# Swapping two buffers in SBUF, and moving split rests, block differences and half-row squares between engines, in a two-layer decoder trunk

## The chip, the cores and the metric

The kernel runs on one core of a Trainium2 chip. The metric is device time in microseconds (us) of one execution; a kernel is run several times and the median is taken. Engines are called by the names that the profile's rows use: PE is TensorE, DVE is VectorE, ACT is ScalarE, POOL is GpSimd, SP is SyncE, which here only issues DMA transfers.

## The reference

x is 1024 tokens by 1024 features in float32. Two layers follow each other; the attention functions themselves are left out here.

```python
def rmsnorm(x, g):
    y = x32 * lax.rsqrt(jnp.mean(x32 * x32, axis=-1, keepdims=True) + RMS_EPS)
    return y * g

def swiglu(h, w_up, w_down):                     # hidden size 2816
    a, b = jnp.split(h @ w_up, 2, axis=-1)
    return (jax.nn.silu(a) * b) @ w_down

for layer in range(2):
    h = rmsnorm(x, norm_mix[layer])
    if layer == 0:                               # "A": compressed + selected + sliding window branches
        mix = nsa_attention(h, a_w_in, ..., a_w_out, rel_bias)
    else:                                        # "B": three (window, dilation) groups, shared K and V
        kv = rmsnorm(x, kv_norm) @ kv_w          # reshaped to three dilations, K and V, 4 groups of 64
        mix = dilated_attention(h, b_w_q, k_shared, v_shared, b_w_out, rel_bias)
    x = x + mix
    x = x + swiglu(rmsnorm(x, norm_ffn[layer]), ffn_w_up[layer], ffn_w_down[layer])
return rmsnorm(x, final_norm)
```

There are 16 heads of 64, in 4 groups. The dilated attention has queries for three dilations (1, 4, 16), all projected from the stream after layer 0.

## The kernel before, in words

**Numbers in two parts.** Every large product is taken on float32 values that are split in two: a rounded high part and the rest. `Pairs` (L993 to L1004) makes such a pair: ScalarE copies the high part (`ph`, L1002), and VectorE, or another engine that is passed as `eng`, subtracts it from the source (`pl`, L1003). `split` does the same into given tiles (L348, L349). A product is then three matmuls (`mm3`, L375 to L377): high by high, and the two mixed ones.

**Products in blocks.** The dense matrices are multiplied in 2 by 2 blocks of 512 with seven products instead of eight. `Blocks` holds the seven left operands made of the normalised stream, transposed and split: B11, B21 (first half of the rows), T1 to T4 and B22 (sums and differences of blocks). `Blocks.factor` gives a row's reciprocal root mean square: the first 512 columns are squared and summed by ScalarE (L1103), the second 512 by VectorE (L1104), then the two sums are added. `Blocks.half` (from L1128) scales the rows, and `make` (L1157 to L1178) forms T1 to T4, with differences by `minus` (L1163), whose even rows go to VectorE and odd rows to GpSimd. `cols_steps` (from L1199) gives the seven products m1 to m7 of one weight block: each splits its weights by `pairs` and multiplies them by one operand; m1 uses B11, m2 B21, m5 T1, m6 T2, m7 T3, m4 T4 and m3 B22.

**The dense part of a layer** is `dense` (L1516 to L1534). It keeps the residual stream in `xr`, 128 partitions by 8 rows by 1024 (32 KB of a partition, pool "fx"). `out_proj` (L1295 to L1350) multiplies the attention's output with w_out; its weights k = 4 to 7 are loaded straight into the four upper rows of xr, the others into a pool of their own (`ow`, loads at L1313). When its last first-half step is done, B11 and B21 are allocated in pool "fb" (also 32 KB). `ffn` (L1371) then runs `hidden` for j = 0 to 21, 128 hidden columns each: weights arrive by DMA, GpSimd multiplies them by the norm's gains (L1388), GpSimd forms the block sums (L1236, L1237, L1251, L1253), and the seven products follow; the down projection is accumulated into xr by VectorE (L1061, and L1506 for the last). For the first three j, `eng` is GpSimd in m1 and m2.

**Between the layers.** `project_B` (L1543 to L1668) runs 18 jobs (6 of keys and values, 12 of queries), each again the seven products, on operands made from the stream after layer 0; `begin_B` (L1536) makes the first half of them during the down projection. It uses xr's rows in pairs as space (`chunk`) in which finished queries are split (L351, L352), from where GpSimd's queue writes them to memory (`qB`, L1592). For its first two jobs `eng` is GpSimd.

**The dilated attention** (L1673 to L1916) then opens pools in the places that have come free: T12 (bias tiles), Q1, K1 for the wide dilations, and so on. `load_first` (L1695) loads the first group in three slices, in SyncE's order: T12 (L1730, L1731), then for each slice Q1, K1, V1, Q2, K2, V2 (L1704, L1710, L1712), later Q0, K0, V0 and T0 for the near dilation (dilation 1). L1793 and L1798 are the first products of keys and queries of the wide groups, L1813 those of the near one. After it a merge (L1857 to L1876) adds the three dilations by weight.

**Order.** Inside the attentions a hand-written order is used. The rest is ordered by a scheduler that simulates a timeline, so that instructions of one engine stand in the order that it found; a tile that is placed where another lay waits for the last use of the other.

Of the kernel before, what the change touches and what calls it, by code (L numbers as in the profile page):

```python
# [299 lines left out]
def trunk(ctx, tc, I, out):  # L300
    nc = tc.nc

    def pool(c, name, side="left", space=None):
        if space is not None:
            return c.enter_context(tc.tile_pool(name=name, bufs=1, space=space,
                                                **({} if space is DR else {"reuse_waits": "tile"})))
        return c.enter_context(tc.tile_pool(name=name, bufs=1, side=side, reuse_waits="tile"))
# [785 lines left out]
    class Blocks:  # L1093
# [5 lines left out]
        def factor(self, xt, junk):  # L1099
            lo, hi = slice(0, 512), slice(512, 1024)  # L1100
            ss = cst.tile([128, 2], F32, name="nss2", bufs=8)
            rs = ss[:, 0:1]
            nc.scalar.activation(junk[0], xt[:, lo], AF.Square, accum_out=rs)  # L1103
            nc.vector.tensor_tensor_reduce(out=junk[1], in0=xt[:, hi], in1=xt[:, hi], scale=1.0, scalar=0.0,  # L1104
                                           op0=OP.mult, op1=OP.add, accum_out=ss[:, 1:2])
            nc.vector.tensor_add(rs, rs, ss[:, 1:2])
            nc.scalar.activation(rs, rs, AF.Sqrt, bias=eps, scale=1.0 / D)
            nc.vector.reciprocal(rs, rs)
            return rs
# [48 lines left out]
        def make(self, name):  # L1158
            (a, b), t = self.x1, self.t
            first = lambda j, h: self.xr[:, j, h * 512:(h + 1) * 512]  # L1160

            def minus(o, x, y, j):
                (nc.vector, nc.gpsimd)[j % 2].tensor_sub(o, x, y)  # L1163

            if name == "T1":
                for j in range(4):
                    nc.vector.scalar_tensor_tensor(t[j], first(j, 0), self.less[j], a[j], op0=OP.mult, op1=OP.add)
                self.turned(name, t)
                for j in range(4):
                    minus(a[j], b[j], a[j], j)  # L1170
            elif name == "T2":
                for j in range(4):
                    minus(t[j], b[j], t[j], j)
                self.turned(name, t)
            elif name == "T3":
                self.turned(name, a)
                for j in range(4):
                    nc.vector.scalar_tensor_tensor(a[j], first(j, 1), self.rs[j], t[j], op0=OP.mult, op1=OP.subtract)  # L1178
            else:
                self.turned(name, a if name == "T4" else b)  # L1180
# [114 lines left out]
    def out_proj(c, near, far, B, xr, oT, w, x_src, late):  # L1295
# [38 lines left out]
        def first(k):  # L1334
            def prep():
                a = pairs(oT[:, k, lo])
                for c_ in range(2):
                    split(*ops[k][c_], raw[k][:, c_ * 512:(c_ + 1) * 512])
                return a

            def run(a):
                a = [part(a, t) for t in range(4)]
                for cs in (((0,), (1,)) if k == 0 else ((0, 1),)):
                    products(k, a, range(4), cs)
                if k == 7:
                    for t in range(4, NT):
                        rows(t)
                    cr.close()
                    B.add(pool(c, "fb", far), ("B11", "B21"))
            return step(prep, run)  # L1350

        def later(m, k):
# [18 lines left out]
    def ffn(p, scratch, B, xr, layer):  # L1371
# [27 lines left out]
        def hidden(j, u):  # L1399

            def ahead(f):
                if j == 1:
                    raw[2].clear()
                if 0 < j < NJ - 1:
                    for q in range(3):
                        load_up(j + 1, q)
                return f()

            def tmp(n):
                if n in ("d0", "d1"):  # L1410
                    return u[base + int(n[1])]
                return scratch[15] if (j, n) == (0, "c") else misc[n]

            def done(a, r, C):
                t = u[base + r]
                if a == 0:
                    nc.scalar.activation(t, C, AF.Silu)
                else:
                    nc.vector.tensor_mul(t, t, C)

            base = 2 * (j % 2)
            banks = {0: ("dx2", "uy", "uy"), 1: ("dx3", "ux", "uy")}.get(j, ("ux", "uy", "uy"))
            steps = cols_steps(banks, "m1 m2 m5 m6 m7 m4 m3", pairs, tmp, B.ops, lambda: raw[j], done,
                               eng=nc.gpsimd if j < 3 else None)
            i = 2 if j in (1, 2) else 0
            steps[i] = steps[i][0], lambda f=steps[i][1]: ahead(f)

            def m4(f=steps[5][1]):
                if j == 0:
                    raw[1].clear()  # L1430
                if j + 1 < NJ:
                    for q in range(3 if j else 0, 4):
                        load_up(j + 1, q)
                return f()
            steps[5] = "m4", m4
            return steps
# [79 lines left out]
    def dense(layer, w, x_src, oT, tail, near, far):  # L1516

        lo, hi = slice(0, 512), slice(512, 1024)
        scratch = [oT[:, 4 * b + i, h] for h in (lo, hi) for b in range(2) for i in range(4)]
        with ExitStack() as c:  # L1520
            c.push(open_banks(*[(n,) for n in ("dx0", "dx1", "dx2", "dr0", "dr1", "ux", "dx3", "uy")]))
            B = Blocks()
            xr = pool(c, "fx", far).tile([128, NT, D], F32, name="xr")
            out_proj(c, near, far, B, xr, oT, w, x_src, layer and 7)
            with ExitStack() as cu:
                p = pool(cu, "fu", near)
                with ExitStack() as ch:
                    B.add(pool(ch, "fb2", far), second)
                    last = ffn(p, scratch, B, xr, layer)
                with ExitStack() as ch:  # L1530
                    pz = pool(ch, "fz", far)
                    begin, finish = tail
                    last(pz, *begin(pz, B, xr))
            finish(c, B, xr, scratch)  # L1534
# [8 lines left out]
    def project_B(c, B, xr, scratch):  # L1543
# [97 lines left out]
        def steps(n):  # L1641
            done = tokens_out(n) if jobs[n][0] == "v" else rows_out(n)
            s = cols_steps((("ux", "uy")[n % 2], "dr0", "dr1"),
                           "m1 m2 m6 m5 m7 m4 m3" if n else "m1 m2 m5 m6 m7 m4 m3", pairs, tmp_of(n), B.ops,
                           lambda: raw[n], done, view_of(n), nc.gpsimd if n < 2 else None)

            def third(f=s[2][1]):
                if 0 < n < len(jobs) - 1:
                    load(n + 1)
                return f()  # L1650
            s[2] = s[2][0], third
            return s
# [318 lines left out]
```

## Time and profile before

| what | value |
|---|---|
| median of 3 runs | 2940.07 us (2934.08 to 2941.08) |
| the profiled execution's own time | 2943.19 us |
| its span (first to last instruction) | 2941.4 us |
| granted TensorE clock, mean over the span | 0.986 |
| PE busy | 2827.1 us (96%) |
| DVE busy | 2266.9 us (77%) |
| POOL busy | 1586.8 us (54%) |
| ACT busy | 1509.1 us (51%) |
| moved by DMA | 294.46 MB, 100 GB/s over the span |

Times inside the profile are counted from the start of the span. A row of a timeline gives the start, the duration, engine, line and operation, with "out<-in" by the names of the tiles; in square brackets stands the idle time of the engine ahead of it and what ended that. A row of waits gives engine, operand and line, what released it, and then total us, number and longest. In the operands, h and l mark the high part and the rest. oT and oTb are big buffers (the attention's output, later used in pieces as space for weights), so that many temporary tiles carry these names. The stages of the span in short: attention A to about 700, dense part of layer 0 to about 1440, project_B to about 1847, the dilated attention to about 2175, the dense part of layer 1 to the end.

### The profile page before, as it was taken

Reading aid. Unit: us, or ns where it says so; the run is one execution under the profiler, and the core shown is the slowest. Engines: PE = TensorE matmul, PEld = TensorE weight load, DVE = VectorE, ACT = ScalarE, POOL = GpSimd, SP = SyncE. Lnnn points to the kernel's source line nnn. Section 1 sums busy time; section 2 is a strip of 40 time slices with the busy share of each in tenths; the row PEclk is TensorE's granted clock in tenths of the full one; section 3 lists DMA queues with packets and bytes.
Section 4 is the critical chain, followed back from the end, with each engine's and each line's share of the span. In section 5 each row is a group of like instructions: output and inputs, shape, how many; then the busy total and the mean of one; then the engine's idle time right before and its main releaser. Section 6 shows DMA issues by size and latency. Waiting matters only on the chain.

```text
span 2941.4 us, 43840 instructions
## 1 busy us (share of the span) xinstructions
PE 2827.1 (96%) x14766; PEld 2377.7 (81%) x14766; DVE 2266.9 (77%) x4485; ACT 1509.1 (51%) x3266; POOL 1586.8 (54%) x1804
## 2 busy tenths in 40 slices
PE   7999999999999999999899999699999999999997
PEld 6988999998877888888678788588878778888886
DVE  5441999996588889888866776489975888898887
ACT  5431888886443333333444444589854433333334
POOL 2134777773365555555456786355523655555551
PEclk8999999999999999999999999899999999999999
DMA  6756243202123222321224554766521221112112
GB/s 160 234 160 189 60 109 88 75 10 115 33 75 74 71 65 61 83 61 54 97 93 140 160 164 141 233 198 194 159 88 33 72 61 51 54 50 62 54 43 76
DMA packets 266833, 294.46 MB, mean 100 GB/s; under 512 B 18099, under 2 KB 209475, under 8 KB 266608
## 3 DMA queue, kind: packets, MB, share of 16 engines
q1 hardware_dynamic: 246960, 231.50, 27.2%
q0 software_dynamic: 19648, 60.16, 6.8%
q8 instruction: 117, 1.92, 0.3%
q14 instruction: 108, 0.88, 0.1%
HBM read 228.49 MB, written 78.81 MB: 104 GB/s over the span
## 4 chain that ended last, share of the span: by engine, by line
PE 69%; DVE 16%; ACT 4%; issue 4%; DMA 4%; POOL 3%; SPq 1%; DVEq 0%; POOLq 0%; ACTq 0%
PE ux L375 5%; PE ux L376 5%; PE ux L377 5%; DVE pl L1003 5%; PE pt L485 4%; PE uy L375 4%; PE uy L376 4%; PE uy L377 4%; DVE xr L1061 4%; PE dx L376 3%; PE dx L377 3%; PE dr L375 3%; PE dx L375 3%; PE dr L376 3%; PE mm L375 3%
## 5 line engine op out<-in xcount | busy, mean ns | idle before, releaser
L1003 DVE TENSOR_TENSOR pl<-oT,ph 128x512 fp32r<-128x512 f32 x315 | 314.9, 1019 | 74.8 <-ACT ph L1002 69.0
L1002 ACT ACTIVATE ph<-oT 128x512 fp32r<-128x512 f32 x325 | 196.4, 626 | 219.3 <-PE ux L376 59.9
L485 PE MATMUL pt<-ident,P 128*128 128x128 f32 x1536 | 260.0, 277 | 5.1 <-DVE tl L349 2.5
L1003 DVE TENSOR_TENSOR pl<-oTb,ph 128x512 fp32r<-128x512 f32 x229 | 216.8, 971 | 52.0 <-ACT ph L1002 47.1
L1002 ACT ACTIVATE ph<-oTb 128x512 fp32r<-128x512 f32 x235 | 140.6, 625 | 189.9 <-PE ux L376 52.4
L1061 DVE TENSOR_TENSOR xr<-xr,dr 128x512 f32<-128x512 f32 x320 | 204.5, 678 | 27.9 <-PE dr L377 27.9
L1388 POOL TENSOR_TENSOR oT<-oT,gffn 128x512 f32<-128x512 f32 x92 | 108.7, 1188 | 199.9 <-DMA oT<-in_ffn_w_up_dram 185.1
L349 DVE TENSOR_TENSOR tl<-pt,th 128x512 fp32r<-128x512 f32 (+1 forms) x320 | 194.2, 625 | 15.4 <-ACT th L348 13.3
L485 PEld LDWEIGHTS pt<-ident,P 128*128 128x128 f32 x1536 | 181.4, 141 | 28.3 <-POOL P L924 4.1
L924 POOL TENSOR_SCALAR P<-P,sm,gates 128x384 f32<-128x384 f32 (+7 forms) x256 | 182.7, 724 | 37.8 <-DVE sm L922 31.8
L1061 DVE TENSOR_TENSOR xr<-xr,dx 128x512 f32<-128x512 f32 x320 | 200.0, 678 | 2.5 <-PE dx L377 1.8
L348 ACT ACTIVATE th<-pt 128x512 fp32r<-128x512 f32 (+1 forms) x320 | 168.4, 546 | 40.0 <-PE pt L485 31.0
L1388 POOL TENSOR_TENSOR oTb<-oTb,gffn 128x512 f32<-128x512 f32 x92 | 103.8, 1136 | 151.6 <-DMA oTb<-in_ffn_w_up_dram 135.6
L920 ACT ACTIVATE P<-P,m 128x384 f32<-128x384 f32 (+7 forms) x256 | 171.1, 671 | 12.5 <-DVE m L918 9.0
L376 PE MATMUL dx<-pl,ph 128*128 128x512 f32 x384 | 152.7, 398 | 0.9
L1762 ACT ACTIVATE P<-P,st 128x384 f32<-128x384 f32 (+2 forms) x256 | 139.5, 548 | 26.1 <-DVE st L1757 25.1
L377 PE MATMUL dx<-ph,pl 128*128 128x512 f32 x384 | 149.9, 393 | 0.4 <-DVE pl L1003 0.4
L1757 DVE CUSTOM_DVE_ANT_0 P<-s,T 128x384 f32<-128x384 f32 (+2 forms) x256 | 115.6, 478 | 37.8 <-PE s L1798 26.9
L510 PE MATMUL o<-tl,V 128*128 128x256 f32 x476 | 135.8, 302 | 0.0
L509 PE MATMUL o<-th,V 128*128 128x256 f32 x476 | 135.1, 298 | 0.2 <-DVE oTb L522 0.2
L375 PE MATMUL dx<-ph 128*128 128x512 f32 x384 | 117.2, 398 | 6.7 <-DVE xr L1506 4.9
L1002 ACT ACTIVATE ph<-wd 128x512 fp32r<-128x512 f32 x86 | 53.8, 629 | 115.7 <-PE ux L376 55.0
(924 smaller groups left out, 9546.1 us busy)
## 6 DMA issues: line engine op xcount, KB each, us to landing
qB<-xr POOLq DMA_DIRECT2D x96, 256.0 KB, 4.7
oT<-in_ffn_w_up_dram SPq DMA_DIRECT2D x92, 256.0 KB, 3.1
oTb<-in_ffn_w_up_dram SPq DMA_DIRECT2D x92, 256.0 KB, 3.1
Q<-qB SPq DMA_DIRECT2D x40, 512.0 KB, 7.3
wd<-in_ffn_w_down_dram SPq DMA_DIRECT2D x66, 256.0 KB, 2.6
oT<-in_b_w_q_dram SPq DMA_DIRECT2D x48, 256.0 KB, 3.3
K<-kBs SPq DMA_DIRECT2D x40, 256.0 KB, 9.6
wraw<-in_a_w_in_dram SPq DMA_DIRECT2D x18, 512.0 KB, 4.7
```

The lines of the kernel that those rows point to most:

```text
L348: nc.scalar.activation(H_, src, AF.Copy)
L349: nc.vector.tensor_sub(L_, src, f32(H_))
L375: nc.tensor.matmul(ps, lh, rh, start=first, stop=False, skip_group_check=bool(shared))
L376: nc.tensor.matmul(ps, lh, rl, start=False, stop=False, skip_group_check=bool(shared))
L377: return nc.tensor.matmul(ps, ll, rh, start=False, stop=last, skip_group_check=bool(shared))
L485: nc.tensor.transpose(ps[:, i * 128:(i + 1) * 128], b, ident)
L920: nc.scalar.activation(P[:, e, :n], P[:, e, :n], AF.Exp, bias=mm[:, e:e + 1], scale=-1.0, accum_out=sm[:, e:e + 1])
L924: nc.gpsimd.tensor_scalar(P[:, e, :n], P[:, e, :n], sm[:, e:e + 1], gt(g, t, br, 2 * hp + e, 1), op0=OP.mult, op1=OP.mult)
L1002: nc.scalar.activation(like(h), src, AF.Copy)
L1003: (eng or nc.vector).tensor_sub(like(l), src, f32(like(h)))
L1061: nc.vector.tensor_add(xs, xs, banks[t])
L1388: nc.gpsimd.tensor_mul(v, v, gains[:, k:k + 4].unsqueeze(2).to_broadcast([128, 4, 128]))
```

## The change

It has five edits. (1) `factor` squares both halves of a row on ScalarE. (2) `minus` uses VectorE for all rows; 12 differences of a run move from GpSimd. (3) In `hidden` for j = 0 to 2 and in (4) `project_B` for n = 0 and 1, the rests of m1's and m2's weights are made by VectorE as everywhere else: 16 operations, 12 of them in the two ffn parts. (5) Pool "fb" with B11 and B21 is opened in `dense` ahead of "fx" and no longer in `out_proj`, so that the two 32 KB regions change places. In layer 0 (right side) xr goes from byte 163392 of a partition to 130624 and B11/B21 the other way; in layer 1 (left side) xr goes from 50496 to 83264. In the dilated attention T12, Q1 and K1 lie from 165440 to 196160, Q0 and K0 from about 130240.

```diff
@@ -1101,8 +1101,7 @@
             ss = cst.tile([128, 2], F32, name="nss2", bufs=8)
             rs = ss[:, 0:1]
             nc.scalar.activation(junk[0], xt[:, lo], AF.Square, accum_out=rs)
-            nc.vector.tensor_tensor_reduce(out=junk[1], in0=xt[:, hi], in1=xt[:, hi], scale=1.0, scalar=0.0,
-                                           op0=OP.mult, op1=OP.add, accum_out=ss[:, 1:2])
+            nc.scalar.activation(junk[1], xt[:, hi], AF.Square, accum_out=ss[:, 1:2])
             nc.vector.tensor_add(rs, rs, ss[:, 1:2])
             nc.scalar.activation(rs, rs, AF.Sqrt, bias=eps, scale=1.0 / D)
             nc.vector.reciprocal(rs, rs)
@@ -1160,7 +1159,7 @@
             first = lambda j, h: self.xr[:, j, h * 512:(h + 1) * 512]
 
             def minus(o, x, y, j):
-                (nc.vector, nc.gpsimd)[j % 2].tensor_sub(o, x, y)
+                nc.vector.tensor_sub(o, x, y)
 
             if name == "T1":
                 for j in range(4):
@@ -1346,7 +1345,6 @@
                     for t in range(4, NT):
                         rows(t)
                     cr.close()
-                    B.add(pool(c, "fb", far), ("B11", "B21"))
             return step(prep, run)
 
         def later(m, k):
@@ -1420,8 +1418,7 @@
 
             base = 2 * (j % 2)
             banks = {0: ("dx2", "uy", "uy"), 1: ("dx3", "ux", "uy")}.get(j, ("ux", "uy", "uy"))
-            steps = cols_steps(banks, "m1 m2 m5 m6 m7 m4 m3", pairs, tmp, B.ops, lambda: raw[j], done,
-                               eng=nc.gpsimd if j < 3 else None)
+            steps = cols_steps(banks, "m1 m2 m5 m6 m7 m4 m3", pairs, tmp, B.ops, lambda: raw[j], done)
             i = 2 if j in (1, 2) else 0
             steps[i] = steps[i][0], lambda f=steps[i][1]: ahead(f)
 
@@ -1520,6 +1517,7 @@
         with ExitStack() as c:
             c.push(open_banks(*[(n,) for n in ("dx0", "dx1", "dx2", "dr0", "dr1", "ux", "dx3", "uy")]))
             B = Blocks()
+            B.add(pool(c, "fb", far), ("B11", "B21"))
             xr = pool(c, "fx", far).tile([128, NT, D], F32, name="xr")
             out_proj(c, near, far, B, xr, oT, w, x_src, layer and 7)
             with ExitStack() as cu:
@@ -1642,7 +1640,7 @@
             done = tokens_out(n) if jobs[n][0] == "v" else rows_out(n)
             s = cols_steps((("ux", "uy")[n % 2], "dr0", "dr1"),
                            "m1 m2 m6 m5 m7 m4 m3" if n else "m1 m2 m5 m6 m7 m4 m3", pairs, tmp_of(n), B.ops,
-                           lambda: raw[n], done, view_of(n), nc.gpsimd if n < 2 else None)
+                           lambda: raw[n], done, view_of(n))
 
             def third(f=s[2][1]):
                 if 0 < n < len(jobs) - 1:
```

Removed lines shift the later ones: the numbers after the change are smaller by one from L1105 on, by two from L1348, by three from L1423 to L1520, and by two behind that.

SyncE at the start of the dilated attention, with what each load waits for (DMAHW and DMASW are counters of transfers issued by SyncE and by GpSimd, the others of engines; oT is the last weight load of project_B; s1 and s2 hold bias in memory). Before:

```order
L1568 DMA oT_2477<-in_b_w_q_dram 128x4x128 [waits DMAHW2_49,DVE_49]
L1682 DMA rows_19095<-in_rowsel_dram 128x512 [waits DMAHW3_49,PE_49]
L1730 DMA T120_19103<-s1_80 128x256 [waits DMASW4_49,DMASW5_49,DMASW3_49,DMASW6_49,DMASW2_49,DMASW7_49,DMASW1_49,DMAHW4_49,DMASW0_49,DVE_49]
L1731 DMA T120_19103<-s2_81 128x128 [waits DMAHW5_49]
L1730 DMA T121_19106<-s1_80 128x256 [waits DMAHW6_49]
```

The same place after the change:

```order
L1566 DMA oT_2477<-in_b_w_q_dram 128x4x128 [waits DMAHW2_49,DVE_49]
L1728 DMA T120_19103<-s1_80 128x256 [waits DMAHW3_49,PE_49]
L1729 DMA T120_19103<-s2_81 128x128 [waits DMAHW4_49]
L1728 DMA T121_19106<-s1_80 128x256 [waits DMAHW5_49,PE_49]
L1729 DMA T121_19106<-s2_81 128x128 [waits DMAHW6_49]
```

The first bias load waited for GpSimd's eight counters, that is for the last writes of qB, and for VectorE's last split into xr; now it waits for a matmul. The counter numbers resolve to the last job's m1 (`uy<-B11`) for T120 and T121; Q10 to Q13 wait for two further reads of B11 and for older writes of qB; V10 waits for the last `pl<-oT` on VectorE, and Q0 for the last writes of qB. The load of `rows` stands behind the first group's key slices. In layer 0's dense part the first w_out load waits for the last product of the attention instead of an earlier one; in layer 1's, the four loads of w_out into xr wait for GpSimd's last L1876.

VectorE at the end of layer 0 (dx_15273 is a sum of the second last down projection into xr, dx_15717 and on those of the last; xn and nss are a row's scratch and its sum of squares). Before:

```order
L1061 TENSOR_TENSOR xr<-xr,dx_15273 128x512
L1003 TENSOR_TENSOR pl<-oT,ph 128x512 x3
L1419 TENSOR_TENSOR oT<-oT 128x512
L1003 TENSOR_TENSOR pl<-s_16151,ph 128x512
L1003 TENSOR_TENSOR pl<-oT,ph 128x512
L1506 TENSOR_TENSOR xr<-xr,dx_15717 128x512
L1506 TENSOR_TENSOR xr<-xr,dx_15725 128x512
L1506 TENSOR_TENSOR xr<-xr,dx_15734 128x512
L1506 TENSOR_TENSOR xr<-xr,dx_15742 128x512
L1104 ISA xn_15685,nss_15793<-xr 128x512
L1104 ISA nss_15793 128x1
L1506 TENSOR_TENSOR xr<-xr,dx_15751 128x512
```

After:

```order
L1061 TENSOR_TENSOR xr<-xr,dx_15273 128x512
L1003 TENSOR_TENSOR pl<-oT,ph 128x512 x3
L1417 TENSOR_TENSOR oT<-oT 128x512
L1003 TENSOR_TENSOR pl<-oT,ph 128x512 x4
L1003 TENSOR_TENSOR pl<-s_16151,ph 128x512
L1003 TENSOR_TENSOR pl<-oT,ph 128x512
L1503 TENSOR_TENSOR xr<-xr,dx_15717 128x512
L1503 TENSOR_TENSOR xr<-xr,dx_15725 128x512
L1503 TENSOR_TENSOR xr<-xr,dx_15734 128x512
L1503 TENSOR_TENSOR xr<-xr,dx_15742 128x512
L1105 TENSOR_TENSOR nss_15793<-nss_15793 128x1
L1503 TENSOR_TENSOR xr<-xr,dx_15751 128x512
```

The four rests that GpSimd made for project_B's first two jobs stand in VectorE's queue ahead of the last sums into xr, and behind the sums the square of the first row is gone.

GpSimd in the first ffn steps of layer 0 (gffn is the norm's gain, tb and wd are space for sums, here of T1's rows). Before:

```order
L1388 TENSOR_TENSOR oT<-oT,gffn_72 128x512
L1003 TENSOR_TENSOR pl<-oT,ph 128x512 x6
L1163 TENSOR_TENSOR tb<-oT,tb 128x512
L1251 TENSOR_TENSOR oT<-oT 128x512
L1163 TENSOR_TENSOR wd_10439<-oT,wd_10439 128x512
L1253 TENSOR_TENSOR oT<-oT 128x512
```

After:

```order
L1235 TENSOR_TENSOR oT<-oT 128x512
L1236 TENSOR_TENSOR oT<-oT 128x512
L1386 TENSOR_TENSOR oT<-oT,gffn_72 128x512
L1250 TENSOR_TENSOR oT<-oT 128x512
L1252 TENSOR_TENSOR oT<-oT 128x512
```

The six rests and the differences of `minus` are gone from GpSimd's queue; what is left are gains and block sums. On VectorE the rests stand right behind the scaling of the second half of the rows, ahead of the operations that form T1, and the transposes of T1 stand 12 to 18 matmuls later in TensorE's order. ScalarE's second squares stand right behind the first ones.

## The prediction

> **What bounds the kernel now.** First the page's head and busy shares, then TensorE's own list of waits (engine, waiting operand and line, releaser: total us, times, longest).
>
> ```profile
> span 2941.4 us, 43840 instructions
> PE 2827.1 (96%) x14766; PEld 2377.7 (81%) x14766; DVE 2266.9 (77%) x4485; ACT 1509.1 (51%) x3266; POOL 1586.8 (54%) x1804
> ```
>
> ```profile
> PE s L1793 <- DMA K<-kBs: 18.1, 2, 17.6
> PE s L1798 <- DMA K<-kBs: 3.5, 4, 2.4
> PE dx L375 <- ACT ow00h L348: 3.1, 1, 3.1
> PE o L509 <- POOL thp L502: 2.8, 3, 2.3
> PE dx L1120 <- DVE T1l L349: 2.1, 1, 2.1
> ```
>
> TensorE is busy for 96% of the span: the change takes no matmul away, so all it can win is the 114 us in which TensorE isn't busy, and the time in which it is busy at a low clock. One wait is large: 17.6 us on the first keys of layer 1's dilated attention. The windows place the waits (stretch, us, then busy us of PE, PEld, DVE, ACT, POOL, the granted clock PEclk, the DMA share, GB/s).
>
> ```profile
> 700.00:704.00 4.00, 3.56 (x10) 2.78 (x11) 4.00 (x8) 3.22 (x7) 0.00 (x0) 0.64 0.98 386
> 1430.00:1440.00 10.00, 4.76 (x19) 3.61 (x19) 10.00 (x9) 1.35 (x3) 8.02 (x5) 0.92 0.10 30
> 1439.20:1445.20 6.00, 5.98 (x14) 4.71 (x15) 4.19 (x10) 3.71 (x8) 2.24 (x3) 0.50 0.58 218
> 1460.00:1490.00 30.00, 24.46 (x119) 18.88 (x118) 27.55 (x46) 14.26 (x28) 14.87 (x12) 0.94 0.21 71
> 1845.00:1865.00 20.00, 2.30 (x9) 1.41 (x7) 2.11 (x4) 3.99 (x6) 4.13 (x8) 0.66 0.68 204
> 2270.00:2290.00 20.00, 15.51 (x80) 11.74 (x79) 19.26 (x25) 11.52 (x20) 13.51 (x10) 1.00 0.18 53
> ```
>
> 1845 to 1865 is the start of the dilated attention: every engine is nearly idle. 1430 to 1440 (end of layer 0), 1460 to 1490 (norms of project_B) and 2270 to 2290 (first steps of layer 1's ffn) are the other kind: VectorE is busy throughout, GpSimd beside it, and TensorE loses 5.2, 5.5 and 4.5 us.
>
> **The swap at the start of the dilated attention.** SyncE's list of waits, SyncE's issues, and the work around them (start us, us, engine, line, operation):
>
> ```profile
> SPq L1730 <- DMA qB<-xr: 18.5, 3, 16.8
> ```
>
> ```profile
> 1823.84 0.39 PE L375 MATMUL uy<-B11h,ph 128*128 128x512 f32 x1
> ...
> 1848.43 2.08 POOL L1592 DMA_DIRECT2D qB<-xr  x4 [1.39 <-ACT xr L351]
> ...
> 1854.77 0.34 SPq L1730 DMA_DIRECT2D T<-s  x1
> ...
> 1858.47 1.85 SPq L1704 DMA_DIRECT2D Q<-qB  x4
> ...
> 1864.39 0.55 PE L1793 MATMUL s<-K,Q 128*128 128x256 f32 x1 [17.64 <-DMA K<-kBs]
> ```
>
> Before, the tiles of T12, Q1 and K1 lie where xr lay, and project_B uses xr's rows as the space from which it writes the finished queries (qB) to memory until the last job. So SyncE stands at its first load until the last write has landed: 1854.77. After, the same tiles lie where B11 and B21 lay. These are last read by the last job's m1 and the product behind it, around 1823.84 to 1826; six more products follow. SyncE then issues T12, Q1 and K1 from about 1824, 30 us earlier. The first value slice follows the last split of the last job, since it lies in the old oT; it, the second group's queries and their first key slice still come before the end of project_B's matmuls. What waits for all qB writes is now Q0, in xr's new place, near the end of that list. The row select load goes behind these too; it was no releaser.
>
> So the 17.64 us go nearly whole. What is late next? The first 16 units' own pace and the near group's bias tile T0, whose load is at the end of the list:
>
> ```profile
> L1793 PE MATMUL s<-K,Q x64: 278/290/580, 1864.4 to 1906.3; 128*128 128x256 f32 x64
> ...
> L1793 PE MATMUL s<-K,Q x64: 276/282/367, 2010.2 to 2053.4; 128*128 128x256 f32 x64
> ```
>
> ```profile
> 1897.14 10.45 DMA T<-sA
> ```
>
> ```profile
> DMA packets 13631, 15.30 MB, mean 251 GB/s; under 512 B 1425, under 2 KB 11025, under 8 KB 13626
> ```
>
> The first wide group took 41.9 us, a later one that waits for no first load 43.2 with other work between: the pace is the kernel's own, so the group moves as a block, and the 17.6 us are kept if T0 comes earlier by as much. It landed at 1907.6 (1897.14 + 10.45), after 15.3 MB at 251 GB/s from 1854 to 1915. With the issue 30 us earlier, less some 9 us in which SyncE stands at the first values, and with the last qB writes in the same queues, I put T0 at 1885 to 1892. That is 16 to 22 us earlier: low end 16. High end 25: the 17.6, the 3.5 and 2.8 us of the two other waits of that attention's start in the list (later keys, T0 by way of GpSimd's thp), and about 1 us for first matmuls at a granted clock of 0.66. I take 20.5: the 17.6 and a little under half of those 6.3 us.
>
> **The swap elsewhere.** At the dense part of layer 0 the first w_out load moves from an earlier matmul's end to that of the attention's last products (matmul, cast that needs the load, group of those loads with KB each and median us from issue to landing):
>
> ```profile
> 695.65 0.28 PE L510 MATMUL o<-tl,V 128*128 128x256 f32 x1
> ```
>
> ```profile
> 699.77 0.61 ACT L348 ACTIVATE ow00h<-ow 128x512 fp32r<-128x512 f32 x1
> ```
>
> ```profile
> ow<-in_a_w_out_dram SPq DMA_DIRECT2D x4, 512.0 KB, 4.2
> ```
>
> 695.93 plus 4.2 is 700.1 against a cast at 699.77, which waits for something else by then; the next three loads go out right behind instead of later. I take 0, bounds 0 and +0.5. At layer 1, xr's new place is under the merge of the three dilations, and four weight loads into it wait for GpSimd's last merge addition:
>
> ```profile
> 2166.45 7.17 POOL L1876 TENSOR_TENSOR oTb<-oTb,o 128x512 f32<-128x512 f32 x4 [2.41 <-DVE oTb L1865]
> ```
>
> ```profile
> 2192.28 0.39 PE L375 MATMUL dx<-ow40h,ph 128*128 128x512 f32 x1
> ```
>
> ```profile
> xr<-in_b_w_out_dram SPq DMA_DIRECT2D x4, 512.0 KB, 5.1
> ```
>
> They are out at 2173.6, land near 2179 and are first used at 2192.28: some 13 us of cover, 0. Without that cover it would cost the 5.1 us of one landing.
>
> **The engine moves.** Sixteen rests and twelve differences go from GpSimd to VectorE, 24 second half-row squares from VectorE to ScalarE. Prices (groups: count, busy us, mean ns): VectorE and GpSimd rests side by side at the end of layer 0, VectorE's rest with GpSimd quiet, and in layer 1's first ffn steps a square on VectorE and the rests on GpSimd.
>
> ```profile
> L1003 DVE TENSOR_TENSOR pl<-oT,ph 128x512 fp32r<-128x512 f32 x4 | 6.1, 1563 | 0.0
> ```
>
> ```profile
> L1003 POOL TENSOR_TENSOR pl<-oT,ph 128x512 fp32r<-128x512 f32 x4 | 6.8, 1727 | 0.0
> ```
>
> ```profile
> L1003 DVE TENSOR_TENSOR pl<-wd,ph 128x512 fp32r<-128x512 f32 x3 | 2.0, 687 | 0.0
> ```
>
> ```profile
> L1104 DVE CUSTOM_DVE_ANT_0 oTb<-xr 128x512 f32<-128x512 f32 x2 | 3.6, 1786 | 0.0
> ```
>
> ```profile
> L1003 POOL TENSOR_TENSOR pl<-oTb,ph 128x512 fp32r<-128x512 f32 x5 | 7.5, 1519 | 17.0 <-PE dr L376 15.5 <-ACT ph L1002 1.6
> ```
>
> A rest takes 0.69 us on VectorE alone and 1.56 beside one of GpSimd: 0.87 for each that meets one. So a moved operation costs VectorE 0.69 and gives up to 0.87 back.
>
> End of layer 0 (VectorE's last residual additions, the matmul that waits for them, ScalarE's first half-row square):
>
> ```profile
> 1438.49 2.47 DVE L1506 TENSOR_TENSOR xr<-xr,dx 128x512 f32<-128x512 f32 x4
> ```
>
> ```profile
> 1439.22 0.79 PE L375 MATMUL dx<-ph 128*128 128x512 f32 x1 [4.87 <-DVE xr L1506]
> ```
>
> ```profile
> 1439.20 0.63 ACT L1103 ACTIVATE xn<-xr 128x512 f32<-128x512 f32 x1 [3.09 <-DVE xr L1506]
> ```
>
> Ahead of the additions at 1438.49, VectorE's four rests at 1.56 become eight at 0.69: 5.5 us instead of 6.3. The two other operations there shed part of their 0.87 each. Bounds -2.5 (both wholly) and +2.75 (four at 0.69 and nothing shed); I take -1.5, since GpSimd keeps two operations there. From 1440 to 1490, eight squares leave VectorE (at 0.69 or more: -5.5), four differences come (+2.75), four differences on GpSimd no longer collide (to -3.5): some 6 us earlier for T1, whose wait is one of those in the 5.5 us that TensorE is idle there. I take -3.3, bounds 0 and -5.5. Sum **-4.8**.
>
> First ffn steps: in 2270 to 2290 two squares at 1.79 leave VectorE (-3.6), five rests and four differences come (9 x 0.69 = +6.2), and nine collisions go (to -7.8): -5.2 on VectorE, and TensorE has 4.5 us to give there. I take -2 in layer 1 and, since layer 0 shows no T1 wait of that size, -1 in layer 0: **-3**, bounds +5 (nothing shed, both layers) and -6.
>
> ScalarE's 24 squares cost 0.63 each and lie where it is busy half of the time (14.26 of 30 us). In layer 0's first norms two squares in line instead of side by side add 0.63 per row, 2.5 over four rows:
>
> ```profile
> 751.54 0.48 DVE L1141 TENSOR_SCALAR oT<-xr,nss 128x512 f32<-128x512 f32 x1
> ...
> 756.60 0.27 PE L1120 MATMUL ux<-ident,oT 128*128 128x128 f32 x1
> ```
>
> The scaled row is there at 752.0, its transpose comes at 756.60: 4.6 us of cover, so 0; uncovered it would be 2.5.
>
> Sum: -20.5 -4.8 -3 = -28.3. The profiled execution took 2943.2 us (span 2941.4); 2943.2 - 28.3 = 2914.9. The median of the runs, 2940.1, lies 3.1 below it, so I forecast 2912.
>
> **The rivals.** (1) The loads, not the distance, bound the start. For it: the DMA share is 0.68 in the very 20 us of the gap, the same bytes must still pass, and SyncE still stands for the values. If bulk loading starts effectively only when that stand ends, the end of the list moves by 12 us instead of 20.5, and with 1 to 3 us from the engine moves the time is 2925 to 2928. Against it: all that the first products need stands in the list ahead of the values. Chance 0.22.
>
> (2) The clock. A gap of 3.1 us (ow00h) is followed by a granted clock of 0.64 over 700 to 704, one of 4.87 us by 0.50 over 1439.2 to 1445.2. If the gap at 1439, shortened to 3.4 us, left the clock full, the six half-clock us there would shrink by 3: 2909. The 0.64 after only 3.1 us speaks against it. Chance 0.08.
>
> The Trainium skill (TensorE: Matmul & The Clock Gate, Part 1: The HAM clock gate) puts the fall to half clock behind at least one idle window of about 3.4 us; by that the shortened gap stands just at the edge, and the trace's 3.1 us gap disagrees.
>
> (3) VectorE becomes the bound, and the kernel is slower. It is busy for 19.26 of 20 us in the first ffn steps. If collisions with GpSimd's remaining operations persist, each of the 28 moved operations costs 1.75 us in front of TensorE, 49 us; the squares give 24 x 0.69 = 16.6 back: +32, less 20.5, is 2952. It is slower than before from 1.33 us for each moved operation ((20.5 + 16.6) / 28). Against it: those collisions are with the very operations that leave. Chance 0.04.
>
> (4) The change doesn't do what it says: SyncE stands, in order, at another load for old qB writes or at Q0, and the keys come as late as before. Then only the engine moves are left: 2940.1 - 8 = 2932, or, with those at half, 2936. Chance 0.04.
>
> **How the numbers follow.** The forecast case has 0.62: its own terms reach from -18 (16, 1.5, 0.5) to -38 (25, 7, 6), 2902 to 2922. With (1) the range goes to 2928; a little below 2902 takes in (2): 2899 to 2928. About 0.3%, 9 us, is what a measurement of this kernel can tell from no change. Faster by more than that: forecast, (1), (2), 0.92; within: (4), 0.04; slower: (3), 0.04.
>
> **What would show it.** Right: SyncE's first T12 load at about 1824 instead of 1854.77; the first product of the dilated attention within 3 us of the end of project_B, with no wait for keys above 3 us and a granted clock near 1 there; the near group 16 to 25 us earlier; gap at the end of layer 0 near 3.4 us. Wrong: that wait still above 8 us, or a new one of TensorE for T0 (GpSimd's select) or for VectorE's rests (pl) in the first ffn steps; a wait for w_out at 700 that grows past 3.6; layer 1's w_out landing after 2192 less the gain.

## The result and the profile after

The changed kernel takes 2913.3 us (median of 4 runs, 2908.86 to 2918.47) against 2940.57 us before (4 runs): 27.3 us less, ratio 0.9911 with a 95% interval of 0.9888 to 0.9934. The forecast was 2912. The profiled execution took 2908.86 us, the fastest of the four, 34.3 us less than the profiled one of before; both traces are single executions, so the trace overstates the gain by some 7 us, and how much of it is clock has to be kept apart.

The first and third line of the page of after:

```profile
span 2907.1 us, 43848 instructions
PE 2817.1 (97%) x14766; PEld 2371.2 (82%) x14766; DVE 2260.1 (78%) x4465; ACT 1522.0 (52%) x3314; POOL 1541.3 (53%) x1776
```

The span is 34.3 us shorter. TensorE's busy time fell by 10.0 us (2827.1 to 2817.1) with the same 14766 matmuls, and the mean granted clock rose from 0.986 to 0.993; its idle time fell by 24.3 us (114.3 to 90.0). TensorE's waits in after:

```profile
PE s L1791 <- DMA K<-kBs: 3.3, 1, 3.3
PE dx L375 <- ACT ow00h L348: 3.1, 1, 3.1
PE o L509 <- POOL thp L502: 2.9, 3, 2.4
...
PE dr L375 <- DVE xr L1061: 2.8, 2, 2.0
...
PE dx L375 <- DVE xr L1503: 2.1, 1, 2.1
...
PE s L1796 <- DMA K<-kBs: 2.0, 2, 1.8
```

The 18.1 us for the first keys are down to 3.3, and the 3.5 us for keys in the next row of products (L1798 before, L1796 after) to 2.0. The wait of 4.9 us at the end of layer 0 is 2.1. The waits for w_out (3.1) and for T0 by way of GpSimd's thp (2.9) stand as before. One wait has grown: that for a residual addition (L1061) is 2.8 us where it was 1.7, and its longest, early in layer 0's ffn, 2.0 where it was 0.8.

SyncE's issues, TensorE's first products and a step of the chain of waits, all of after, at the start of the dilated attention:

```profile
1810.88 0.34 SPq L1728 DMA_DIRECT2D T<-s  x1
...
1814.71 1.75 SPq L1702 DMA_DIRECT2D Q<-qB  x4
...
1819.91 0.38 SPq L1710 DMA_DIRECT2D V<-vBs  x1
```

```profile
1832.75 0.39 PE L377 MATMUL dr<-B22h,pl 128*128 128x512 f32 x1
1832.97 0.88 PE L1791 MATMUL s<-K,Q 128*128 128x256 f32 x6
```

```profile
1866.80 10.44 DMA T<-sA
```

SyncE issues the first bias load 21.9 us ahead of project_B's last matmul, where it stood 8 us behind it before, and the first product of keys and queries follows that last matmul at once. T0 lands at 1877.24. Windows of after, by stage:

```profile
700.00:704.00 4.00, 4.00 (x19) 3.33 (x18) 3.58 (x7) 2.58 (x5) 0.00 (x0) 1.00 1.02 404
1426.00:1436.00 10.00, 6.67 (x25) 4.07 (x26) 10.00 (x17) 3.96 (x9) 5.73 (x3) 1.00 0.09 26
...
1456.00:1486.00 30.00, 28.90 (x143) 23.55 (x142) 29.28 (x49) 17.93 (x36) 8.36 (x8) 0.89 0.21 70
...
1833.00:1848.00 15.00, 10.24 (x71) 9.74 (x70) 8.12 (x24) 11.12 (x27) 5.04 (x10) 0.89 0.90 289
2238.00:2258.00 20.00, 18.34 (x98) 14.39 (x97) 18.20 (x27) 12.06 (x21) 7.03 (x6) 1.00 0.18 53
```

At the end of layer 0 VectorE does 17 operations in 10 us where it did 9, and TensorE is idle 3.3 us instead of 5.2. In project_B's first steps (1456 on) the 5.5 us of idle are 1.1. In layer 1's first ffn steps 4.5 us of idle are 1.7.

### The profile page after: what moved, and what is told of

It is laid out like the page before. It is cut to its first block, busy times and chain, and to the rows that moved or that the text cites. A ratio compares the mean times of both kernels' runs of the same rounds, so it can differ in the third digit from the quotient of the medians.

```text
span 2907.1 us, 43848 instructions
## 1 busy us (share of the span) xinstructions
PE 2817.1 (97%) x14766; PEld 2371.2 (82%) x14766; DVE 2260.1 (78%) x4465; ACT 1522.0 (52%) x3314; POOL 1541.3 (53%) x1776
## 4 chain that ended last, share of the span: by engine, by line
PE 70%; DVE 16%; ACT 4%; issue 4%; DMA 3%; POOL 3%; SPq 1%; DVEq 0%; ACTq 0%; POOLq 0%
PE ux L375 5%; PE ux L376 5%; PE ux L377 5%; PE pt L485 5%; DVE pl L1003 5%; PE uy L375 4%; PE uy L376 4%; DVE xr L1061 4%; PE uy L377 4%; PE dx L376 3%; PE dx L377 3%; PE dr L375 3%; PE dx L375 3%; PE mm L375 3%; PE dr L376 3%
## 5 line engine op out<-in xcount | busy, mean ns | idle before, releaser
L1003 DVE TENSOR_TENSOR pl<-oT,ph 128x512 fp32r<-128x512 f32 x325 | 324.1, 1018 | 71.2 <-ACT ph L1002 61.9
L1061 DVE TENSOR_TENSOR xr<-xr,dr 128x512 f32<-128x512 f32 x320 | 204.5, 678 | 27.6 <-PE dr L377 27.6
L1061 DVE TENSOR_TENSOR xr<-xr,dx 128x512 f32<-128x512 f32 x320 | 199.9, 677 | 2.5 <-PE dx L377 1.8
```

The costliest lines, as they stand in the source:

```text
L1003: (eng or nc.vector).tensor_sub(like(l), src, f32(like(h)))
L1061: nc.vector.tensor_add(xs, xs, banks[t])
```

## The experiments

The theory is that the terms of the prediction add up (the swap at the start of the dilated attention, the engine moves at the end of layer 0 and in the first ffn steps). The rivals that were worth a run: the swap is all of it; the start is bound by the bytes that have to be loaded; of the engine moves one edit carries the gain; the edits trade one wait for another.

### The swap alone

```diff
             B = Blocks()
+            B.add(pool(c, "fb", far), ("B11", "B21"))
...
                     cr.close()
-                    B.add(pool(c, "fb", far), ("B11", "B21"))
```

> Only edit (5): pool fb ahead of fx; every engine move left as before. Theory (terms add up): the whole gain at the start of the dilated attention is the swap's, the first product of keys and queries follows project_B's last matmul within about 3 us, and nothing else moves: 18 us less than before, about 2922, with the gap of 4.9 us at the end of layer 0 still there. Rival A (the swap is nearly the whole change and the engine moves give nothing): 27 us less, about 2913. Rival B (the start is bound by the bytes to be loaded): the first product comes early, but the near group's first product only 12 us earlier, about 2928.

Measured: 2918.9 us, ratio 0.9921 (0.9909 to 0.9934): 21 us less by the medians, 23 by the ratio. Its page and its waits:

```profile
span 2914.1 us, 43853 instructions
PE 2820.5 (97%) x14766; PEld 2375.8 (82%) x14766; DVE 2269.8 (78%) x4485; ACT 1509.2 (52%) x3266; POOL 1585.6 (54%) x1804
```

```profile
PE dx L375 <- DVE xr L1505: 4.9, 1, 4.9
PE o L509 <- POOL thp L502: 4.0, 3, 3.5
PE s L1793 <- DMA K<-kBs: 3.2, 1, 3.2
```

The gap at the end of layer 0 is the old one, the wait for keys the new one. What the swap is worth in its own stage can be read without the rest: from project_B's last matmul to the last product of the near group (L1813 in before, L1811 in after: the source view gives first and last start).

```profile
L1813 PE MATMUL s<-K,Q x256: 274/283/562, 1910.5 to 2151.8; 128*128 128x256 f32 x128
```

```profile
L1813 PE MATMUL s<-K,Q x256: 274/282/562, 1883.6 to 2125.4; 128*128 128x256 f32 x128
```

```profile
L1811 PE MATMUL s<-K,Q x256: 274/283/470, 1879.9 to 2120.2; 128*128 128x256 f32 x128
```

Before, with the last matmul at 1846.36, that is 305.4 us; with the swap alone (last matmul at 1836.40) 289.0; in after (1832.75) 287.5. The swap gives 16.4 to 18 us there. The near group's first product stands 47.2 us behind project_B's last matmul where it stood 64.1, so it comes 16.9 us earlier and not 12: rival B falls. Rival A (nearly everything is the swap) is not borne out, since the moves without the swap give 8 us, next. The 21 to 23 us of the whole runs are 3 to 7 more than the stage shows; no place was found for these.

### The engine moves without the swap

All of the change but edit (5); the diff is that of the change without its two "fb" lines.

> Edits (1) to (4) without the swap. Theory: 9 us less at the end of layer 0 and in project_B's first steps, 3 less in layer 1's first ffn steps, 3 more in layer 0's first ffn steps: about 9 us less than before, 2931, with the 17.6 us wait for keys unchanged. Rival A: no difference beyond 3 us, 2938 to 2943. Rival C (VectorE becomes the bound where GpSimd's work is added): slower than before, 2945 or more.

Measured: 2932.4 us, ratio 0.9971 (0.996 to 0.9982): 8 us less. Its largest wait of TensorE:

```profile
PE s L1791 <- DMA K<-kBs: 17.5, 2, 16.8
```

The wait for keys is untouched. Rivals A and C fall. The theory's sum is right here, but the next six runs show that its parts aren't. This run also gives the swap's price a second time, with the moves on both sides: from project_B's last matmul (1833.54) to the last near product (2141.4) it takes 307.9 us for 287.5 in after, so 20.4 in the stage, and by the medians 19 (2932.4 to 2913.3).

### Squares, rests and differences, one by one and in pairs

```diff
-            nc.vector.tensor_tensor_reduce(out=junk[1], in0=xt[:, hi], in1=xt[:, hi], scale=1.0, scalar=0.0,
-                                           op0=OP.mult, op1=OP.add, accum_out=ss[:, 1:2])
+            nc.scalar.activation(junk[1], xt[:, hi], AF.Square, accum_out=ss[:, 1:2])
```

> Edit (1) alone: both half-row squares on ScalarE. Theory: VectorE's time ahead of the transposes of T1 sets the wait in project_B's first steps, so without eight squares there it gives about 4 us between 1440 and 1490, and 2 in layer 1's first ffn steps; the 4.9 us gap at 1439 stays: 2934. Rival D (the collisions with GpSimd matter, not VectorE's own work): no more than 2 us, 2938 to 2942.

```diff
-            steps = cols_steps(..., done, eng=nc.gpsimd if j < 3 else None)
+            steps = cols_steps(..., done)
...
-                           lambda: raw[n], done, view_of(n), nc.gpsimd if n < 2 else None)
+                           lambda: raw[n], done, view_of(n))
```

> Edits (3) and (4) alone: the 16 rests on VectorE. Theory: the gap of 4.9 us at the end of layer 0 falls by 3 us; in the first ffn steps the rests lengthen VectorE's queue ahead of T1 by 2 to 3 us in each layer, since the squares are still there: about 2 us more to 1 us less, 2939 to 2942. Rival D (collisions matter): VectorE is quicker everywhere, 3 us less in each of three places, about 2931.

```diff
-                (nc.vector, nc.gpsimd)[j % 2].tensor_sub(o, x, y)
+                nc.vector.tensor_sub(o, x, y)
```

> Edit (2) alone: all differences on VectorE. Theory E (of the engine moves, squares and rests alone gave nothing, the two moved together with the differences gave 8 us, so one edit carries it): minus alone gives about 8 us, 2932. Theory I (the three edits work only together, since each alone only trades VectorE's own work against collisions): 0 to 2 us, 2938 to 2941.

The three pairs put two of these edits together each.

> Edits (1), (3) and (4): squares on ScalarE and rests on VectorE, differences shared as before. Theory I: the two are complements (the rests shorten the gap at the end of layer 0 by 3 us, the squares make room for them ahead of T1): 5 to 6 us less than before, about 2934. Theory E: nothing without the differences, 2939 to 2942.

> Edits (1) and (2): squares on ScalarE, differences on VectorE, rests as before. Theory I: project_B's first steps and layer 1's first ffn steps gain 3 us each, the gap at 1439 stays: about 2935. Theory E: all of the 8 us, 2932.

> Edits (2), (3) and (4): differences and rests on VectorE, squares on VectorE too. Theory I: VectorE has 28 operations more and no relief; the gap at 1439 shrinks by 3 us, T1 comes later in three places by 2 us each: 2940 to 2944. Theory E: 8 us less, 2932.

Measured, with two sums of TensorE's waits beside each: the gap at the end of layer 0 (for xr, L1503 to L1506) and all waits for T1's rests (T1l).

| moved | median us | ratio to before (95%) | gap | T1l |
|---|---|---|---|---|
| nothing | 2940.1 to 2940.6 | 1 | 4.9 | 3.6 |
| squares | 2940.3 | 0.9998 (0.9988 to 1.0007) | 4.9 | 3.9 |
| rests | 2942.4 | 1.0005 (0.9996 to 1.0014) | 2.1 | 8.3 |
| differences | 2942.2 | 1.0012 (1.0002 to 1.0022) | 4.9 | 5.8 |
| squares, rests | 2931.8 | 0.9976 (0.9966 to 0.9986) | 2.1 | 1.5 |
| squares, differences | 2942.1 | 1.0008 (1.0 to 1.0017) | 4.9 | 5.0 |
| rests, differences | 2942.5 | 1.0008 (0.9999 to 1.0018) | 2.1 | 8.5 |
| all three | 2932.4 | 0.9971 (0.996 to 0.9982) | 2.1 | 2.1 |

Squares and rests give nothing alone and 8 us together; the differences give nothing in any company and are slower by 0.1% alone, by an interval that just clears 1. For squares alone the theory's 2934 is missed and rival D's 2938 to 2942 holds; for rests alone it is the other way round (2942.4, at the edge of the theory's 2939 to 2942 and far from D's 2931), so neither VectorE's own work nor the collisions account for both. Theory E falls. Theory I holds for two of the pairs (with squares and rests it gave 5 to 6 us, and they are 8) and fails for squares with differences (2935). The two columns on the right show most of why: together they fall from 8.5 to 3.6 us with squares and rests, which is 4.9 of the 8 us, and they rise by 0.3 to 2.2 us in every row that gives nothing. Rows of the waits, of squares alone, rests alone and the pair:

```profile
PE dr L1119 <- DVE T1l L349: 3.1, 2, 1.6
```

```profile
PE dr L1120 <- DVE T1l L349: 6.5, 2, 3.3
```

```profile
PE dr L1119 <- DVE T1l L349: 1.1, 2, 0.6
```

(Two waits each, one in each ffn.) The rests, moved alone, shorten the gap by 2.8 us, but in the ffn they stand in VectorE's queue ahead of T1, together with the squares: the wait for T1 is 3.3 us in each layer, where before it was 1.5 in layer 1 and none in layer 0. The squares, moved alone, leave layer 1's wait where it was and add one of 1.6 in layer 0, which eats what they take from project_B's (2.1 to 0.8). VectorE in layer 1's first ffn steps before (L1104 is a square, L1167 one of the operations of `make` that form T1's rows):

```profile
2265.82 1.77 DVE L1104 CUSTOM_DVE_ANT_0 oTb<-xr 128x512 f32<-128x512 f32 x1
...
2267.60 0.74 DVE L1167 SCALAR_TENSOR_TENSOR oTb<-xr,less,ta 128x512 f32<-128x512 f32 x1
```

The same place with the squares alone (L1105 adds a row's two sums of squares, L1166 is L1167 of before), and GpSimd's rests beside it:

```profile
2265.54 1.01 DVE L1105 TENSOR_TENSOR nss<-nss 128x1 f32<-128x1 f32 x1 [1.42 <-ACT wd L1103]
2266.57 1.77 DVE L1166 SCALAR_TENSOR_TENSOR oTb<-xr,less,ta 128x512 f32<-128x512 f32 x1
...
2270.10 1.70 DVE L1166 SCALAR_TENSOR_TENSOR oTb<-xr,less,tb 128x512 f32<-128x512 f32 x1
```

```profile
2262.27 8.98 POOL L1003 TENSOR_TENSOR pl<-oTb,ph 128x512 fp32r<-128x512 f32 x6 [17.40 <-ACT ph L1002]
```

And with squares and rests:

```profile
2257.76 0.74 DVE L1166 SCALAR_TENSOR_TENSOR oTb<-xr,less,ta 128x512 f32<-128x512 f32 x1
...
2258.49 0.74 DVE L1166 SCALAR_TENSOR_TENSOR oTb<-xr,less,tb 128x512 f32<-128x512 f32 x1
```

Without its two squares VectorE first stands 1.42 us for ScalarE's, and then goes through T1's operations at the pace that GpSimd's six rests set: 1.77 and 1.70 us for what takes 0.74 when GpSimd is quiet. That takes back nearly all of the 3.6 us that two squares are worth (1.42, 1.03 and 0.96). Take the rests from GpSimd as well and both reasons are gone (T1l 0.6 for 1.6).

### The change without its differences

The change with `minus` as before, that is edits (1), (3), (4) and (5); it is called no_minus from here on.

```diff
-                nc.vector.tensor_sub(o, x, y)
+                (nc.vector, nc.gpsimd)[j % 2].tensor_sub(o, x, y)
```

> Edits (1), (3), (4) and (5): the change without edit (2), so the odd rows' differences stay on GpSimd. Theory I (squares and rests are complements, the differences give nothing, the swap adds to them): 21 to 23 less from the swap and 8 to 9 less from the pair, 2909 to 2912. Rival F (with the swap the differences do count): 2916 or more.

Measured: 2917.5 us (4 runs, 2911.73 to 2919.88), ratio 0.9913 (0.99 to 0.9927): the same as the change (0.9911) within the intervals. So no effect of edit (2) is seen with the swap either, as theory I has it; but the level, 2917.5, lies in rival F's range, by the medians it is 4.2 us more than the change, and the intervals, some 4 us to either side, don't exclude an effect of that size. With 21 to 23 from the swap and 8 from the pair 2909 to 2912 was expected. The ratio against the swap alone is better by only 0.0008, 2 us, where it was 8 us without the swap; the intervals (each 4 us to either side) just let both be true. One reading is that the six runs of the swap alone came out some us low: with 16 to 20 us for it, as its stage and the comparison with the moves on both sides have it, and 8 for the pair, the sum is 24 to 28, and 0.9913 is 26 us. That isn't settled.

### T0 ahead of Q0

No_minus, with two lines changed round (called t0_first):

```diff
                     if r == 1:
-                        load(0, g)
                         load_T0(g)
+                        load(0, g)
```

> As no_minus, and in every group the four loads of T0 stand ahead of those of Q0, K0 and V0 in SyncE's order. Theory G (the near group's start waits for T0 by its place at the end of the list only): the 2.4 us wait on GpSimd's thp goes, 2 us less than no_minus, about 2908. Rival B (the bytes bound the start: the same bytes must be there before the near group can go on): a wait for queries, keys or values takes its place, the same time as no_minus within 1 us or up to 2 more.

Measured: 2906.0 us (2903.77 to 2907.04), ratio 0.9876 (0.9861 to 0.9891): 11 us less than no_minus by the medians, the fastest kernel of the study. Five times what theory G gave, and rival B's time is missed. The groups of loads (KB each, median us from issue to landing) of no_minus and of this kernel:

```profile
T<-sA SPq DMA_DIRECT2D x5, 128.0 KB, 6.5
```

```profile
T<-sA SPq DMA_DIRECT2D x5, 128.0 KB, 2.3
```

Two windows of 20 us around the start of the near group, again no_minus and this kernel:

```profile
1865.00:1885.00 20.00, 17.14 (x147) 16.66 (x145) 15.23 (x46) 16.30 (x47) 10.08 (x22) 1.00 0.93 266
1885.00:1905.00 20.00, 18.98 (x128) 17.46 (x129) 12.89 (x50) 16.04 (x50) 10.99 (x22) 0.83 0.97 286
```

```profile
1859.00:1879.00 20.00, 19.11 (x160) 18.35 (x158) 15.77 (x49) 17.76 (x53) 12.92 (x27) 1.00 0.92 259
1879.00:1899.00 20.00, 19.33 (x155) 17.74 (x155) 17.60 (x71) 19.22 (x63) 10.12 (x20) 1.00 0.96 275
```

And the row of no_minus for T0, of which this kernel has 0.6 us left in two waits of 0.3:

```profile
PE o L509 <- POOL thp L502: 3.0, 3, 2.4
```

TensorE issues 160 and 155 matmuls where it issued 147 and 128, at the same rate of bytes (259 and 275 GB/s for 266 and 286): what was late is the bias tiles of 128 KB that everything of the near group waits for, behind 2 MB of queries, and not the bytes as a whole. The 2.4 us wait on thp is gone, and with it a granted clock of 0.83. No wait for loads takes its place behind the changed order; the largest one of this kernel, 4.1 us for values at 1846.2, comes ahead of it, where no_minus has 3.1 for keys. From project_B's last matmul to the last near product it is 283.6 us (1834.65 to 2118.2) against 288.6 (1840.77 to 2129.4): 5.0 us of the 11 lie there. The five traces that have the swap and T0 last take 287.5 to 289.5 for the stage, so 4 to 6 us stand against all of them. The other 6 were not found in one place: the two traces differ by 6.1 us ahead of project_B's end, where every engine does the same instructions in the same order in both kernels, so that part is chance, and the two ratios leave anything from 3 to 19 us for the whole.

```profile
L1811 PE MATMUL s<-K,Q x256: 274/283/562, 1886.6 to 2129.4; 128*128 128x256 f32 x128
```

```profile
L1811 PE MATMUL s<-K,Q x256: 274/283/472, 1877.2 to 2118.2; 128*128 128x256 f32 x128
```

### The rests in one place only

No_minus with `eng` back in `hidden`, so that only project_B's four rests are moved:

```diff
             steps = cols_steps(banks, "m1 m2 m5 m6 m7 m4 m3", pairs, tmp, B.ops, lambda: raw[j], done,
+                               eng=nc.gpsimd if j < 3 else None)
```

> As no_minus, but the ffn's first rests stay on GpSimd; only project_B's four are moved. Theory I: the gap at the end of layer 0 is 2.1 us as in the change (8 us less there), both ffn parts keep a T1 wait of 1.5 to 2 us and lose about 3 in layer 0 and 2 in layer 1 against no_minus: 2914 to 2916. Rival H (the pair's gain lies wholly at the end of layer 0): as no_minus, 2909 to 2912.

And with `eng` back in `project_B`, so that only the ffn's twelve are moved:

```diff
-                           lambda: raw[n], done, view_of(n))
+                           lambda: raw[n], done, view_of(n), nc.gpsimd if n < 2 else None)
```

> As no_minus, but project_B's four rests stay on GpSimd; only the ffn's twelve are moved. Theory I: the 4.9 us gap at the end of layer 0 is back with half clock behind it, 4 to 5 us more than no_minus: 2914 to 2916. Rival J (the gap is made up later in project_B's steps): 2909 to 2912.

Measured: 2921.0 us, ratio 0.9926 (0.9914 to 0.9939), and 2916.8 us, 0.9915 (0.9901 to 0.9928). Their waits, first the one with project_B's rests moved, then the one with the ffn's:

```profile
PE dr L1119 <- DVE T1l L349: 3.1, 2, 1.6
PE dx L375 <- DVE xr L1504: 2.1, 1, 2.1
```

```profile
PE dx L375 <- DVE xr L1503: 4.8, 1, 4.8
PE dr L1119 <- DVE T1l L349: 1.1, 2, 0.6
```

The waits go just where the rests went: the gap shrinks with project_B's four, the ffn's T1 waits with the ffn's twelve. The times are less clear than the waits. The expected ranges started from a no_minus at 2909 to 2912, so they are compared with its measured 2917.5 instead. With only project_B's rests it is 3.5 us more than no_minus by the medians, for theory I's 5 and rival H's nothing, but within the intervals, so neither is shown. With only the ffn's rests the 4 to 5 us more of theory I are not there: either the longer gap is made up later (rival J) or the scatter hides it, and that stays open.

## Why the prediction was right

**The total** came out at -27.3 us for -28.3, and the shares of its two big parts hold: -21 to -23 for the swap alone, -19 beside the moves (forecast -20.5), and -8 for the moves alone (forecast -7.8).

**The swap's mechanism** is the one described. The first load was put at about 1824 in before's time; project_B ended 13.6 us earlier in after, and 1824 less 13.6 is 1810.4, measured 1810.88. T0 was put at 1885 to 1892; 1877.24 plus 13.6 is 1890.9. The 17.6 us ahead of the first product are gone whole. That T0 lies in its range is luck in part. It was worked out with some 9 us in which SyncE stands at the first values. In after, SyncE's wait there is 0.9 us:

```profile
SPq L1710 <- DVE pl L1003: 0.9, 1, 0.9
```

Instead the list from the first queries to T0 took 52.1 us (1814.71 to 1866.80) where it took 38.7 before (1858.47 to 1897.14). Why it took longer isn't shown.

**What of it was mis-sized**: "half of those 6.3 us", the later waits for keys and T0. In after, keys are waited for twice, 3.3 and 2.0 us, and T0's 2.9 is as before: none of the half is gone. The first keys' wait above 3 us, given as a sign against, is there by 0.3 us. The clock was better at the start, 0.89 in after's window where the window of the gap had 0.66, but the first wide group was not quicker for it: from the first product of keys and queries to the near group's first it is 46.1 us before and 46.9 in after. So the stage gave the 17.6 us and little else in these two traces (18.0 in all).

**Rival 1** (the loads bound the start) was right that loads still come late, but the end of the list moved by 16.7 us in before's time (T0 at 1890.9 for 1907.6) and not by 12. The run with T0 first shows that T0's place in the order costs 4 to 6 us, which the working took as given.

**The engine moves: right sum, wrong parts.** That -7.8 met -8 is luck. The failing step is "a moved operation costs VectorE 0.69 and gives up to 0.87 back", added up edit by edit. It priced the four differences in project_B's first steps as a gain (+2.75 against -3.5), and moving the differences alone costs 0.1%. It priced the squares as -5.5 there and -3.6 in layer 1, and alone they give nothing. The terms don't add: in the rows of layer 1, VectorE is late by its own queue or by its pace beside GpSimd, and only the pair takes away both. One term stands by itself, the gap at the end of layer 0: put at -1.5 with a bound of -2.5, it is -2.8 (4.9 to 2.1) in all eight traces in which project_B's rests are moved, and in no other.

**The first ffn steps** were put at -2 in layer 1 and -1 in layer 0. Layer 1's idle time fell from 4.5 to 1.7 us per 20 (-2.8). Layer 0 shows the grown wait of 2.0 us for a residual addition (0.8 before) and a T1 wait of 0.7 where before had none, so no gain is seen there. Without the differences the wait for the addition is 0.8 again, and the median isn't lower; so it isn't settled as a cost.

**The covers held**: the wait for w_out at 700 is 3.1 us in both, and neither layer 1's w_out nor layer 0's row norms appear among the larger waits.

**Rival 2** (the clock stays full behind a shorter gap) came true in after's profiled run, by another way: the gap fell to 2.1 us, not 3.4, and the window behind it was granted 1.00. That is no property of the kernel; the last section shows the same gap with half clock behind it.

## What to carry to other kernels

When a stage boundary stalls on first loads, look at what the destination tiles covered before, not only at where the load stands in its queue: swapping two equal regions, so that the new tiles lie on the one that dies first, bought 16 to 20 us in its stage for one moved line. Then look at the order of that list, since 128 KB tiles that everything needs, behind 2 MB of queries, held up another 4 to 6 us by the traces and 11 by the medians. And price engine moves together: two edits that give nothing alone may each be waiting for the other.

## What the runs showed of the hardware that was not expected

The granted clock behind the same gap differs from run to run. Behind the gap of 2.1 us at the end of layer 0, after and then t0_first:

```profile
1436.00:1439.40 3.40, 3.40 (x15) 2.79 (x16) 3.07 (x6) 3.38 (x9) 2.00 (x4) 1.00 0.64 231
```

```profile
1437.90:1441.30 3.40, 3.40 (x10) 2.62 (x9) 2.43 (x7) 3.37 (x10) 1.59 (x2) 0.50 0.52 209
1441.30:1447.00 5.70, 5.70 (x29) 4.67 (x28) 4.06 (x13) 4.99 (x14) 1.06 (x2) 1.00 0.42 166
```

In t0_first the half clock holds for 3.4 us and is then full at once: 10 matmuls in 3.4 us, where after has 15. The wait of 3.1 us for w_out at 700 is in both lists, and the window of 700 to 704 was granted 0.64 in before and 1.00 in after. Over the 14 traces of before, after and the twelve experiments, the clock fell to half at or just behind the gap of 2.1 us in 3 of the 8 that have it, at the one of 3.1 us in 6 of 14, and at the one of 4.8 to 4.9 us in 6 of 6; it stayed down for 3.4 or 6.8 us. The Trainium skill (TensorE: Matmul & The Clock Gate, Part 1: The HAM clock gate) has the clock fall after at least one idle window of about 3.4 us. Here it fell behind gaps of 2.1 and 3.1 us, in some executions and not in others, so a short gap can cost an estimated 1.7 us more (half of 3.4) or nothing. Single executions of one kernel differ by 10 us and more (2908.86 to 2918.47 in after, with mean granted clocks of 0.993 and 0.989; 2927.92 to 2940.52 in ten runs of the moves alone). With some ten runs of a kernel the interval was still 3 us to either side, and one trace against another told of chance as much as of the edit.
